# The second MLP product of a hybrid encoder block: seven Strassen block products in place of eight, on one Trainium2 core

## Chip, cores and metric

The kernel runs on one core of one Trainium2 chip. The metric is the device time of one execution in microseconds. Three runs of the kernel before took 856.59, 857.76 and 857.15 us; the median is 857.15 us.

## What is computed

The layer has 512 tokens and 1024 channels. A recurrent mixer and a sparse attention run side by side, their outputs are gated, added and projected, and the result is added to the input. Behind that stands the squared-ReLU MLP, which is what the change is about:

```python
D_MODEL = 1024; SEQ = 512; D_FF = 4 * D_MODEL
...
merged = gates[:, :, 0] * (y_rnn @ w_o_rnn) + gates[:, :, 1] * (y_attn @ w_o_attn)
x = x + merged @ w_out

h2 = rms_norm(x, norm2_w)
x = x + jnp.square(jax.nn.relu(h2 @ w_ff_in)) @ w_ff_out
```

All of it is float32. The second product has 512 x 4096 activations and 4096 x 1024 weights.

## The kernel before

**Precision.** TensorE multiplies in a rounded float32 type (fp32r). Every operand is split into a high part (ScalarE casts it) and a low part (VectorE subtracts the cast from the original), and one product of two operands is three matmuls: high by high, high by low, low by high (mm3, line 443). Weights are split in the same way when they arrive: unit (line 464) loads 128 x 1024 floats into a tile raw, ScalarE casts them into wh, and VectorE (or GpSimd) subtracts into wl. The pools hold 2 tiles raw, 5 wh and 5 wl (SLOTS, line 49).

**Layout.** Channels lie on the partitions and the 512 tokens along the free axis. A block of 128 output channels is one PSUM bank of 128 x 512, and the weights are the stationary operand (block, line 481).

**The MLP** (lines 923 to 947) runs in two halves of the hidden channels. In each half 16 blocks of the first product are made (24 matmuls of 512 columns each), ReLU is taken on ScalarE and the square on VectorE, and the result is split into hidh and hidl. Then for each of the 8 blocks of output channels 48 matmuls run over these 16 hidden blocks, and VectorE scales the bank by the inverse norm (a tile rb2 of 128 x 512) and adds it to x2, the residual. In the second half x2 goes out by DMA after that; its last block is cut into two halves of 256 tokens. The norm of a token is needed for all channels at once, so one fp32 matmul with a matrix of ones (line 935) spreads the sums over all partitions.

**What sets the order.** The program is a list of operations, and a planner (Plan, lines 118 to 339) puts them into one fixed order per engine with its own table of costs and numbers of buffers; each engine then works through its queue in order and waits at semaphores. A buffer is a slot with a tag. The change touches the tags a (67 tiles of 128 x 512), pt (4 tiles of 128 x 1664, which hold the transposed attention weights pth and ptl of a head, line 835), T and S (2 PSUM banks each) and acc (4 PSUM banks). DMAs of weights are issued by SyncE (SP), one after the other in its queue.

**Attention.** For each of 16 heads PE makes the scores, VectorE adds the bias, ScalarE takes the exponentials and the normalisation (norm, line 418), PE transposes the four tiles of weights (flip, line 449), they are cast and subtracted into pth and ptl, and PE multiplies them by the values. Matmuls of other products stand between these steps in PE's queue.

Of the kernel before, what the change touches and what calls it, by code (L numbers as in the profile page):

```python
# [11 lines left out]
F32 = mybir.dt.float32  # L12
F32R = mybir.dt.float32r
# [4 lines left out]
D = 1024  # L18
T = 512
# [325 lines left out]
def build(tc, out, xT, w_x, w_iq, w_vi, w_k, w_q, w_or, w_oa, w_o, w_f1, w_f2, w_bd, vec, nw):  # L345
# [22 lines left out]
    def val(x):  # L368
        return x.real() if isinstance(x, View) else x
# [68 lines left out]
    def mm(o, a, b, first, last, fp32=False):  # L438
        n = o.n
        cost = (4 if fp32 else 1) * n / 2.4 + 13.4 if n > 128 else 86  # L440
        plan.add("pe", cost, lambda: nc.tensor.matmul(val(o), lhsT=val(a), rhs=val(b), start=first, stop=last), [o], [a, b])  # L441

    def mm3(o, a, b, first, last):
        mm(o, a[0], b[0], first, False)
        mm(o, a[0], b[1], False, False)
        mm(o, a[1], b[0], False, last)

    def flip(o, a):
        plan.add("pe", 86, lambda: nc.tensor.transpose(val(o), val(a.f), val(ident)), [o], [a, ident])  # L449
# [28 lines left out]
        sub(l[:, 0:n], raw[:, 0:n], h[:, 0:n], "any")  # L478
        return h, l

    def block(src, x, parts=None, get=unit):

        w = [get(s_) for s_ in src]
        res = []
        for s in parts or [slice(0, T)]:
            o = P()[:, s]
            for k, x_ in enumerate(x):
                u = w[k // KT]
                mm3(o, (u[0][:, tok(k % KT)], u[1][:, tok(k % KT)]), (x_[0][:, s], x_[1][:, s]), k == 0, k == len(x) - 1)
            res.append((s, o))  # L490
        return res if parts else res[0][1]
# [41 lines left out]
    def tok(t):  # L533
        return slice(t * 128, (t + 1) * 128)
# [384 lines left out]
        x2w.append((h, l))  # L919

    rb2 = A("rb2")
    HALF = DFF // 256
    for half in range(2):
        hid = []
        for n in range(half * HALF, half * HALF + HALF):
            o = block([w_f1[n]], x2w)
            r_ = A("rel")
            act(r_, o, AF.Relu)  # L930
# [21 lines left out]
def pack(inputs):  # L952
    a = {k: np.asarray(v) for k, v in inputs.items()}
    w = a["w_in"][0]

    def cols(m):
        n = m.shape[1] // 128
        return m.reshape(KT, 128, n, 128).transpose(2, 1, 0, 3).reshape(n, 128, 1024)

    def rows(m, per):  # L960
        n = m.shape[1]
        return m.reshape(KT // per, per, 128, n).transpose(0, 2, 1, 3).reshape(KT // per, 128, per * n)

# [8 lines left out]
    p = {  # L972
        "xT": a["x"][0].T.reshape(KT, 128, T),
        "w_x": cols(np.concatenate([w[:, 0:2048], w[:, 4168:6216]], axis=1)),
        "w_iq": rows(w[:, 3584:4096], 1),
        "w_vi": rows(np.concatenate([w[:, 3328:3584], w[:, 4096:4168]], axis=1), 8)[0],
        "w_k": rows(w[:, 3072:3328], 4),
        "w_q": cols(w[:, 2048:3072]),
        "w_or": cols(a["w_o_rnn"][0]),
        "w_oa": cols(a["w_o_attn"][0]),  # L980
        "w_o": cols(a["w_out"][0]),
        "w_f1": cols(a["w_ff_in"][0]),
        "w_f2": a["w_ff_out"][0].reshape(4, KT, 128, 8, 128).transpose(3, 0, 2, 1, 4).reshape(8, 4, 128, 1024),
        "w_bd": bd.reshape(2, 128, 1024),
        "vec": np.concatenate([chan(a[k][0]) for k in (
            "norm1_w", "conv_w", "conv_b", "rg_ba", "rg_bx", "rg_lambda", "gate_b", "norm2_w")], axis=1),
        "nw": np.broadcast_to(np.concatenate([a[k][0] for k in ("q_norm_w", "k_norm_w", "idx_k_norm_w")]), (128, 192)),
    }
    return {k: np.ascontiguousarray(v) for k, v in p.items()}
# [11 lines left out]
```

## Time and profile before

| what | before |
|---|---|
| median of 3 runs | 857.15 us |
| the profiled execution, its own time | 856.84 us |
| its span, first to last instruction | 854.7 us |
| PE busy | 841.5 us, 98% |
| DVE (VectorE) busy | 513.9 us, 60% |
| ACT (ScalarE) busy | 440.9 us, 52% |
| DMA | 92.34 MB, mean 108 GB/s |

Shares are means over the whole span. A matmul is listed with its full duration, which overlaps the next one's, so how fast PE goes is read from the distance between two starts and not from durations or busy time. The lines of a helper (441 matmul, 449 transpose, 396 two-input operation of VectorE, 383 and 385 ScalarE) stand for many places in the program; the names of the tiles tell them apart.

### The profile page before, as it was taken

What the parts mean: (1) busy time and instruction counts of PE and PEld (TensorE: products, weight loads), DVE (VectorE), ACT (ScalarE), POOL (GpSimd) and SP (SyncE); (2) the same over time, 40 slices, a digit from 0 to 9 for tenths busy, and PEclk for the clock granted to TensorE, in tenths of its full rate; (3) what the DMA queues carried; (4) which work ended last, traced back from release to release, by engine and by line L of the source; (5) the groups of instructions that cost most, each with busy time, mean ns of one, the idle gap of its engine ahead of it and who ended that gap; (6) DMA issues with size and microseconds to landing.
All of it is one profiled execution on the core that took longest, in us unless ns stands there. A gap on an engine that the chain in (4) does not pass through costs nothing.

```text
span 854.7 us, 10592 instructions
## 1 busy us (share of the span) xinstructions
PE 841.5 (98%) x4004; PEld 703.6 (82%) x4004; DVE 513.9 (60%) x958; ACT 440.9 (52%) x756; POOL 113.2 (13%) x110
## 2 busy tenths in 40 slices
PE   9979999999999999999999999999999999999998
PEld 9968888888788888888788888888888888888887
DVE  7786989899647676857386556444333344443321
ACT  8668697699566575777734333443111244331110
POOL 1552224211031222122040000000000000000000
PEclk9989999999999999999999999999999999999999
DMA  7573778864322412121024332233333333333310
GB/s 264 163 197 81 167 155 194 196 150 119 99 74 74 158 53 74 50 75 49 26 81 140 101 99 96 91 91 96 97 97 99 98 99 99 99 98 124 120 54 25
DMA packets 27986, 92.34 MB, mean 108 GB/s; under 512 B 3232, under 2 KB 3616, under 8 KB 27936
## 3 DMA queue, kind: packets, MB, share of 16 engines
q1 hardware_dynamic: 21024, 66.51, 24.8%
q0 software_dynamic: 6912, 25.17, 13.2%
q8 instruction: 31, 0.51, 0.3%
q14 instruction: 19, 0.16, 0.1%
HBM read 89.57 MB, written 2.10 MB: 107 GB/s over the span
## 4 chain that ended last, share of the span: by engine, by line
PE 95%; ACT 2%; POOL 1%; issue 1%; DVE 1%; POOLq 0%; ACTq 0%
PE ps L441 93%; PE ps L449 2%; ACT xnh L383 0%; POOL wl L396 0%; ACT rel L385 0%; ACT sm L385 0%; ACT ikT L383 0%; POOL bdl L396 0%; DVE iks L396 0%; PE ps L813 0%; POOL cik L396 0%; ACT L385 0%; ACT pth L383 0%; DVE hl L396 0%; POOL wh L460 0%
## 5 line engine op out<-in xcount | busy, mean ns | idle before, releaser
L383 ACT CAST wh<-raw 128x1024 fp32r<-128x1024 f32 (+2 forms) x94 | 98.3, 1048 | 217.7 <-PE ps L441 196.0
L396 DVE TENSOR_TENSOR wl<-raw,wh 128x1024 fp32r<-128x1024 f32 (+1 forms) x91 | 110.8, 1218 | 123.0 <-ACT wh L383 122.2
L441 PE MATMUL ps<-xnh,wl 128*128 128x512 f32 x320 | 126.4, 395 | 0.0
L441 PE MATMUL ps<-xnl,wh 128*128 128x512 f32 x320 | 126.1, 394 | 0.0
L441 PE MATMUL ps<-xnh,wh 128*128 128x512 f32 x320 | 126.0, 394 | 0.0
L441 PE MATMUL ps<-hidl,wh 128*128 128x512 f32 (+1 forms) x272 | 102.4, 377 | 0.0
L441 PE MATMUL ps<-hidh,wl 128*128 128x512 f32 (+1 forms) x272 | 102.4, 377 | 0.0
L441 PE MATMUL ps<-hidh,wh 128*128 128x512 f32 (+1 forms) x272 | 102.4, 377 | 0.0
L441 PE MATMUL ps<-x2h,wh 128*128 128x512 f32 x256 | 100.0, 391 | 0.0
L441 PE MATMUL ps<-x2h,wl 128*128 128x512 f32 x256 | 99.6, 389 | 0.0
L441 PE MATMUL ps<-x2l,wh 128*128 128x512 f32 x256 | 99.6, 389 | 0.0
L441 PEld LDWEIGHTS ps<-xnl,wh 128*128 128x128 f32 x320 | 60.2, 188 | 11.9
L441 PEld LDWEIGHTS ps<-xnh,wl 128*128 128x128 f32 x320 | 60.2, 188 | 11.7
L441 PEld LDWEIGHTS ps<-xnh,wh 128*128 128x128 f32 x320 | 60.2, 188 | 11.3
L396 POOL TENSOR_TENSOR wl<-raw,wh 128x1024 fp32r<-128x1024 f32 (+1 forms) x18 | 45.4, 2523 | 155.2 <-PE ps L441 61.8
L441 PEld LDWEIGHTS ps<-hidh,wl 128*128 128x128 f32 x272 | 51.2, 188 | 9.4
L441 PEld LDWEIGHTS ps<-hidh,wh 128*128 128x128 f32 x272 | 51.2, 188 | 9.4
L441 PEld LDWEIGHTS ps<-hidl,wh 128*128 128x128 f32 x272 | 51.2, 188 | 9.3
L441 PEld LDWEIGHTS ps<-x2h,wh 128*128 128x128 f32 x256 | 48.0, 188 | 10.2 <-issue 0.2
L441 PEld LDWEIGHTS ps<-x2l,wh 128*128 128x128 f32 x256 | 48.1, 188 | 10.1 <-issue 0.2
L441 PEld LDWEIGHTS ps<-x2h,wl 128*128 128x128 f32 x256 | 48.0, 188 | 10.1
L396 DVE TENSOR_TENSOR y<-ps,rb 128x512 f32<-128x512 f32 (+1 forms) x17 | 11.2, 660 | 65.4 <-PE ps L441 65.4
(213 smaller groups left out, 1595.2 us busy)
## 6 DMA issues: line engine op xcount, KB each, us to landing
raw<-w_f SPq DMA_DIRECT2D x64, 512.0 KB, 3.5
wh<-w_x POOLq DMA_DIRECT2D x24, 512.0 KB, 5.1
wl<-w_x POOLq DMA_DIRECT2D x24, 512.0 KB, 5.5
raw<-w_q SPq DMA_DIRECT2D x8, 512.0 KB, 3.6
raw<-w_or SPq DMA_DIRECT2D x8, 512.0 KB, 3.5
raw<-w_x SPq DMA_DIRECT2D x8, 512.0 KB, 3.4
raw<-w_oa SPq DMA_DIRECT2D x8, 512.0 KB, 3.5
raw<-w_o SPq DMA_DIRECT2D x8, 512.0 KB, 3.5
```

The costliest lines, as they stand in the source:

```text
L383: nc.scalar.copy(val(o), val(a))
L396: return lambda: ENG[e].tensor_tensor(val(o), val(a), val(b), op=op)
L441: plan.add("pe", cost, lambda: nc.tensor.matmul(val(o), lhsT=val(a), rhs=val(b), start=first, stop=last), [o], [a, b])
L449: plan.add("pe", 86, lambda: nc.tensor.transpose(val(o), val(a.f), val(ident)), [o], [a, ident])
```

## The change

The first product stays as it is. The second is done in the other orientation and with fewer matmuls.

- The residual x2 is transposed on PE to token-major tiles xt (32 transposes of 128 x 128 into four-wide banks with the tag S, copied out by ScalarE). The inverse norm becomes one column of four numbers per partition (rs2); the ones matmul and the reciprocal of 128 x 512 go.
- The hidden channels are worked in four chunks of 8 blocks, which are 4 pairs (a, b). A pair gives a 2 x 2 grid: rows are token halves H1 and H2, columns are the blocks a and b. Strassen's sums of these quarters (s12, s34) are made on VectorE, and each of them is split into high and low parts. ScalarE now takes the square.
- The weights of a pair come as w_f2 rows (two DMAs into one tile w2 of tag pt, and one into b21 of tag a). Their sums are made in place on VectorE (tt on b12, b11, b21), and each operand is cast and subtracted into wh and wl just before its product (operands).
- A chunk has seven products in the order 1, 2, 6, 5, 7, 3, 4, of 24 matmuls each: 4 pairs, 2 token tiles, 3 matmuls. The activations are stationary, the weights move (512 columns). Each product fills or adds to two PSUM banks (R or V, tag acc), and after each put adds both banks, scaled by rs2, to xt with one VectorE operation per bank. Products 6, 7, 3 and 4 add onto banks that were already read by an earlier put.
- The output is stored token-major, 8 DMAs of 128 x 512 at the end.

```diff
-    rb2 = A("rb2")
-    HALF = DFF // 256
-    for half in range(2):
-        hid = []
-        for n in range(half * HALF, half * HALF + HALF):
-            o = block([w_f1[n]], x2w)
-            r_ = A("rel")
-            act(r_, o, AF.Relu)
-            tt(r_, r_, r_, ALU.mult, "any")
-            hid.append(split(r_, "hid"))
...
-        for c in range(KT):
-            src = [w_f2[c, 2 * half + u] for u in range(2)]
...
-            for s, o in block(src, hid, parts):
-                y_ = A("y2")[:, s]
-                tt(y_, o, rb2[:, s], ALU.mult)
-                tt(x2[c][:, s], x2[c][:, s], y_, ALU.add)
-                if half == 1:
-                    dma(out[c][:, s], x2[c][:, s])
+    xt = [[A("xt") for _ in range(2)] for _ in range(NT)]
+    for t in range(NT):
+        for d in range(2):
+            tp = P("S")
+            for c in range(4):
+                flip(tp[:, tok(c)], x2[4 * d + c][:, tok(t)])
+            act(xt[t][d], tp, either=True)
...
+    for t in range(NT):
+        mm(ss_ps[:, t:t + 1], sacc2[:, tok(t)], ones[:, 0:1], True, True, True)
...
+    def halves(src, cols):
+        h, l = cols
+        act(h, src, either=True)
+        sub(l, src, h)
+
+    def hidden(n):
+        o = block([w_f1[n]], x2w, unit, "T")
+        r_ = A("rel")
+        act(r_, o, AF.Relu)
+        act(r_, r_, AF.Square)
+        return r_
...
+    for ch in range(CHUNKS):
+        S, a22, w = [], [], []
+        for j in range(PAIRS):
+            a, b = (hidden((ch * PAIRS + j) * 2 + i) for i in range(2))
...
+            halves(a[:, H1], at)
+            tt(s12[:, H1], a[:, H2], b[:, H2], ALU.add)
+            tt(s12[:, H2], s12[:, H1], a[:, H1], ALU.subtract)
+            tt(s34[:, H1], a[:, H1], a[:, H2], ALU.subtract)
+            tt(s34[:, H2], b[:, H1], s12[:, H2], ALU.subtract)
+            pb, p12, p34 = two("ab"), two("s12"), two("s34")
+            for src, dst in ((b, pb), (s12, p12), (s34, p34)):
+                halves(src, dst)
...
+            raw = plan.tile(ab, [128, 1664], F32, "pt", "w2")
+            b21 = A("b21")
+            n = (ch * PAIRS + j) * 2
+            dma(raw[:, 0:1024], w_f2[n])
+            dma(b21, w_f2[n + 1][:, 0:512])
+            dma(raw[:, 1024:1536], w_f2[n + 1][:, 512:1024])
...
+        def product(i, o, B, first):
+            for j in range(PAIRS):
+                for p in range(2):
+                    mm3(o[p], cut(S[j][i], tok(p)), B[j], first and j == 0, j == PAIRS - 1, not first)
...
+        def put(i, d, o):
+            left[i, d] -= 1
+            for p in range(2):
+                t, x_ = 2 * i + p, xt[2 * i + p][d]
+                stt(x_, o[p], rs2[:, t:t + 1], x_, ALU.mult, ALU.add)
+                if left[i, d] == 0:
+                    dma(out[t][:, d * 512:d * 512 + 512], x_)
+
+        R, V = banks("acc"), banks("acc")
+        product(1, R, operands(0), True)
+        put(0, 0, R)
+        product(2, V, operands(2), True)
+        put(0, 0, V)
+        for b11, b12, b21, b22, _ in w:
+            tt(b12, b22, b12, ALU.subtract)
+            tt(b11, b12, b11, ALU.add)
+        product(6, R, operands(0), False)
+        put(0, 1, R)
+        for b11, b12, b21, b22, _ in w:
+            tt(b21, b21, b11, ALU.subtract)
+            tt(b11, b22, b11, ALU.subtract)
+        V = banks("acc")
+        product(5, V, operands(0), True)
+        put(1, 1, V)
+        t3b22 = []
...
+        product(7, R, [cut(u, slice(0, 512)) for u in t3b22], False)
+        put(1, 1, R)
+        product(3, V, [cut(u, slice(512, 1024)) for u in t3b22], False)
+        put(0, 1, V)
+        product(4, R, operands(2), False)
+        put(1, 0, R)
```

The planner orders the whole program anew. Three places show what moves.

PE at the last attention head (the last with pth and ptl; ps is a PSUM bank, sm the weights, ya the attention output by which the next product, w_oa, is fed). Before:

```order
L441 MATMUL ps_4278<-yal_3770,wh_3939 128x512
L441 MATMUL ps_4278<-yah_3756,wl_3958 128x512
L441 MATMUL ps_4278<-yah_4016,wh_3939 128x512
L449 MATMUL ps_4318<-ident_72,sm_4153 128x128 [waits DVE_49]
L449 MATMUL ps_4318<-ident_72,sm_4153 128x128 x3
L441 MATMUL ps_4278<-yal_4029,wh_3939 128x512
L441 MATMUL ps_4278<-yah_4016,wl_3958 128x512
L441 MATMUL ps_4278<-yah_4242,wh_3939 128x512
L441 MATMUL ps_4278<-yal_4246,wh_3939 128x512
L441 MATMUL ps_4278<-yah_4242,wl_3958 128x512
L441 MATMUL ps_4330<-pth_4295,vs_482 128x512 [waits Activation_49]
L441 MATMUL ps_4330<-ptl_4301,vs_482 128x512 [waits DVE_49]
```

After, from the end of head 15 of 16 on:

```order
L441 MATMUL ps_4315<-pth_4271,vs_627 128x128
L441 MATMUL ps_4315<-ptl_4280,vs_627 128x128
L450 MATMUL ps_4328<-ident_72,sm_4163 128x128 [waits PE_49,Activation_49]
L450 MATMUL ps_4332<-ident_72,sm_4171 128x128 [waits PE_49,Activation_49]
L450 MATMUL ps_4332<-ident_72,sm_4171 128x128
L450 MATMUL ps_4343<-ident_72,sm_4178 128x128 [waits DVE_49]
L450 MATMUL ps_4343<-ident_72,sm_4178 128x128 x2
L450 MATMUL ps_4348<-ident_72,sm_4187 128x128 [waits DVE_49,Activation_49]
L450 MATMUL ps_4348<-ident_72,sm_4187 128x128 x3
L441 MATMUL ps_4356<-pth_4335,vs_482 128x512 [waits Activation_49]
L441 MATMUL ps_4356<-ptl_4340,vs_482 128x512 [waits DVE_49]
```

Before, matmuls of the next product (ya) stand between the last head's transposes (ident, sm) and its product with the values (vs); after, none stands there: the transposes follow the fifteenth head directly and the product with the values follows them.

PE at the start of the MLP, where the output projection (mg) ends and the first block of the first MLP product (x2h, x2l) begins. Before:

```order
L441 MATMUL ps_4835<-mgl_4582,wh_4677 128x512
L441 MATMUL ps_4835<-mgh_4573,wl_4689 128x512
L441 MATMUL ps_4874<-x2h_4607,wh_4716 128x512 [waits DVE_49,Activation_49]
L441 MATMUL ps_4874<-x2l_4615,wh_4716 128x512
L441 MATMUL ps_4874<-x2h_4607,wl_4728 128x512
L441 MATMUL ps_4874<-x2h_4647,wh_4716 128x512
L441 MATMUL ps_4874<-x2l_4659,wh_4716 128x512
```

After:

```order
L441 MATMUL ps_4877<-mgh_4624,wl_4729 128x512
L450 MATMUL ps_4916<-ident_72,x_196 128x128
L450 MATMUL ps_4916<-ident_72,x_2831 128x128
L450 MATMUL ps_4916<-ident_72,x_2835 128x128
L450 MATMUL ps_4916<-ident_72,x_2955 128x128
L450 MATMUL ps_4922<-ident_72,x_2963 128x128 [waits DVE_49]
L450 MATMUL ps_4922<-ident_72,x_2968 128x128 [waits DVE_49]
L450 MATMUL ps_4922<-ident_72,x_2975 128x128 [waits DVE_49]
L441 MATMUL ps_4926<-x2h_4658,wh_4756 128x512 [waits Activation_49]
L441 MATMUL ps_4926<-x2l_4670,wh_4756 128x512
L441 MATMUL ps_4926<-x2h_4658,wl_4768 128x512
L441 MATMUL ps_4926<-x2h_4687,wh_4756 128x512
```

The first 12 of the 32 transposes of x2 stand there and among the following 25 matmuls of that block; each group of four waits for a bank that ScalarE has to empty.

VectorE late in a chunk. Before, in the second half of the second product (y and x are the scaling and the addition):

```order
L396 TENSOR_TENSOR y_6743<-ps_6676,rb_4957 128x512 [waits PE_49]
L396 TENSOR_TENSOR x_2831<-x_2831,y_6743 128x512 [waits DVE_49]
L396 TENSOR_TENSOR wl_6753<-raw_6697,wh_6739 128x1024 [waits DMAHW2_49,Activation_49]
L396 TENSOR_TENSOR wl_6782<-raw_6725,wh_6774 128x1024 [waits DMAHW3_49,PE_49,Activation_49]
L396 TENSOR_TENSOR y_6808<-ps_6741,rb_4957 128x512 [waits PE_49]
L396 TENSOR_TENSOR x_2837<-x_2837,y_6808 128x512 [waits DVE_49]
L396 TENSOR_TENSOR wl_6818<-raw_6762,wh_6804 128x1024 [waits DMAHW5_49,Activation_49]
L396 TENSOR_TENSOR wl_6847<-raw_6790,wh_6839 128x1024 [waits DMAHW6_49,PE_49,Activation_49]
```

After, in the second chunk from the last split of the operands of products 7 and 3 on (xt rows are put, w is the weight tile of the third chunk, b is b21):

```order
L396 TENSOR_TENSOR wl_6155<-w_5519,wh_6142 128x1024 [waits Activation_49]
L424 SCALAR_TENSOR_TENSOR xt_4991<-ps_6118,rs_4993,xt_4991 128x512 [waits PE_49]
L424 SCALAR_TENSOR_TENSOR xt_5011<-ps_6127,rs_4993,xt_5011 128x512 [waits PE_49]
L396 TENSOR_TENSOR wl_6180<-b_4049,wh_6169 128x512 [waits Activation_49]
L396 TENSOR_TENSOR wl_6180<-b_4055,wh_6169 128x512 [waits Activation_49]
L396 TENSOR_TENSOR w_6124<-w_6124 128x512 [waits DMAHW4_49,DMAHW3_49,DVE_49]
L396 TENSOR_TENSOR w_6147<-w_6147 128x512 [waits DMAHW6_49,DMAHW5_49,DVE_49]
L424 SCALAR_TENSOR_TENSOR xt_4991<-ps_5987,rs_4993,xt_4991 128x512 [waits DVE_49,PE_49]
L424 SCALAR_TENSOR_TENSOR xt_5011<-ps_5993,rs_4993,xt_5011 128x512 [waits DVE_49,PE_49]
L396 TENSOR_TENSOR w_6157<-w_6157 128x512 [waits DMAHW7_49,DMAHW0_49]
L396 TENSOR_TENSOR wl_6219<-b_4066,wh_6212 128x512 [waits Activation_49]
L396 TENSOR_TENSOR wl_6219<-b_4075,wh_6212 128x512 [waits Activation_49]
```

Where before two splits of weights and two operations on a finished bank alternated, there are now splits, puts and sums on weights, and the sums on w wait for DMAs (DMAHW) of the next chunk's weights while puts and splits of the running chunk stand behind them.

In SP's queue the loads of w2 and b21 are issued as soon as slots are free: two w2 tiles before the first heads of the attention, nine b21 tiles in its course, and the next two w2 tiles when the last two heads have released their pt slots, ahead of the last block of w_oa. From the second chunk on the four w2 tiles of a chunk are loaded when the splits for products 7 and 3 of the chunk before have read the old ones.

## Rows read from the trace of the kernel before

**Rows 1.** The page's part 1: busy us of each engine (share of the span) xinstructions.

```profile
PE 841.5 (98%) x4004; PEld 703.6 (82%) x4004; DVE 513.9 (60%) x958; ACT 440.9 (52%) x756; POOL 113.2 (13%) x110
```

**Rows 2.** Chain that ended last: start us, us, what.

```profile
428.07 422.76 PE ps L441 x1907
```

**Rows 3.** Busy us by engine over the MLP: window, length, PE, PEld, DVE, ACT, POOL.

```profile
501.00:851.00 350.00, 349.81 (x1587) 291.09 (x1585) 140.67 (x161) 99.89 (x126) 1.29 (x1) 1.00 0.30 93
```

**Rows 4.** Timeline of PE, 512 columns, then 256: start us, us, engine, what.

```profile
504.82 0.39 PE L441 MATMUL ps<-x2h,wl 128*128 128x512 f32 x1
...
511.62 0.39 PE L441 MATMUL ps<-x2h,wl 128*128 128x512 f32 x1
...
849.58 0.28 PE L441 MATMUL ps<-hidh,wh 128*128 128x256 f32 x1
...
850.53 0.28 PE L441 MATMUL ps<-hidh,wl 128*128 128x256 f32 x1
```

**Rows 5.** Timeline of PE around a group of four transposes, earlier stage.

```profile
79.78 0.60 PE L449 MATMUL ps<-ident,ks 128*128 128x128 f32 x4
...
80.45 0.40 PE L441 MATMUL ps<-xnh,wl 128*128 128x512 f32 x1
```

**Rows 6.** Groups by form: ScalarE's cast of a PSUM bank: busy us, mean ns of one.

```profile
L383 ACT CAST pth<-ps 128x512 fp32r<-128x512 f32 x16 | 9.4, 585 | 3.9 <-PE ps L449 3.7
```

**Rows 7.** Sums of squares on PE: timeline with 512 columns; tile sacc, one column.

```profile
511.84 1.02 PE L441 MATMUL ps<-sacc,ones 128*128 128x512 f32 x2
...
512.93 0.39 PE L441 MATMUL ps<-x2l,wh 128*128 128x512 f32 x1
...
L441 PE MATMUL ps<-ones,sacc x8: 166/250/250, 22.8 to 23.5; 128*128 128x1 f32 x8
```

**Rows 8.** Groups of VectorE by form (tile y: ns min/median/max): mean ns of one.

```profile
L396 DVE TENSOR_TENSOR wl<-raw,wh 128x1024 fp32r<-128x1024 f32 x89 | 108.8, 1223 | 123.0 <-ACT wh L383 122.2 <-PE ps L441 0.6
L396 DVE TENSOR_TENSOR rel<-rel 128x512 f32<-128x512 f32 x32 | 21.9, 685 | 0.0
L396 DVE TENSOR_TENSOR hidl<-rel,hidh 128x512 fp32r<-128x512 f32 x31 | 21.5, 693 | 21.4 <-ACT hidh L383 21.4
L396 DVE TENSOR_TENSOR y<-ps,rb x17: 424/692/692, 600.0 to 850.9; 128x512 f32<-128x512 f32 x15, 128x256 f32<-128x256 f32 x2
L424 DVE SCALAR_TENSOR_TENSOR x2l<-x,vt,x2h 128x512 fp32r<-128x512 f32 x8 | 6.0, 748 | 0.8 <-ACT x2h L385 0.8
```

**Rows 9.** DMA issues: size of one, median us from issue to landing.

```profile
raw<-w_f SPq DMA_DIRECT2D x64, 512.0 KB, 3.5
out<-x SPq DMA_DIRECT2D x7, 256.0 KB, 2.0
out<-x SPq DMA_DIRECT2D x2, 128.0 KB, 1.7
```

**Rows 10.** Timeline of PE between the last two attention heads.

```profile
418.59 0.27 PE L441 MATMUL ps<-ptl,vs 128*128 128x128 f32 x1
...
425.01 0.40 PE L441 MATMUL ps<-pth,vs 128*128 128x512 f32 x1
```

**Rows 11.** Groups by form: the steps of a head between scores and values.

```profile
L418 ACT ACTIVATE sm<-sm,st 128x512 f32<-128x512 f32 x16 | 11.5, 720 | 0.0
L383 ACT COPY yt<-ps 64x512 f32<-64x512 f32 x16 | 9.3, 581 | 16.7 <-PE ps L441 16.7
L396 DVE TENSOR_TENSOR ptl<-ps,pth 128x512 fp32r<-128x512 f32 x16 | 11.0, 688 | 3.4 <-ACT pth L383 3.3
```

**Rows 12.** Timeline of the end: the last bank and the store.

```profile
850.85 0.42 DVE L396 TENSOR_TENSOR y<-ps,rb 128x256 f32<-128x256 f32 x1 [4.87 <-PE ps L441]
851.31 0.42 DVE L396 TENSOR_TENSOR x<-x,y 128x256 f32<-128x256 f32 x1
851.76 0.33 SPq L436 DMA_DIRECT2D out<-x  x1
```

**Rows 13.** A VectorE operation of 512 columns that runs beside GpSimd's work.

```profile
L396 DVE TENSOR_TENSOR qsql<-qsq,qsqh 128x512 fp32r<-128x512 f32 x8 | 7.7, 972 | 1.0 <-ACT qsqh L383 0.9
```

More of the change, by code (lines that the diff above doesn't have):

```diff
@@ L436, in dma, with mm, mm3 @@
         plan.add("sp", n * 128 * 4 / 268.0, lambda: nc.sync.dma_start(val(o), val(src)), w, r)
-    def mm(o, a, b, first, last, fp32=False):
+    def mm(o, a, b, first, last, fp32=False, more=False):
         n = o.n
         cost = (4 if fp32 else 1) * n / 2.4 + 13.4 if n > 128 else 86
[L441 to L446, printed above, removed]
+        plan.add("pe", cost, lambda: nc.tensor.matmul(val(o), lhsT=val(a), rhs=val(b), start=first, stop=last, skip_group_check=more), [o], [a, b])
+    def mm3(o, a, b, first, last, more=False):
+        mm(o, a[0], b[0], first, False, more=more)
+        mm(o, a[0], b[1], False, False, more=more)
+        mm(o, a[1], b[0], False, last, more=more)
     def flip(o, a):
@@ L479, in unit, with block @@
         return h, l
-    def block(src, x, parts=None, get=unit):
+    def block(src, x, get=unit, tag="acc"):
         w = [get(s_) for s_ in src]
[L484 to L491, printed above, removed]
+        o = P(tag)
+        for k, x_ in enumerate(x):
+            u = w[k // KT]
+            mm3(o, (u[0][:, tok(k % KT)], u[1][:, tok(k % KT)]), x_, k == 0, k == len(x) - 1)
+        return o
     def natural(pieces, per, n, x):
@@ new lines, in build @@
+    for t in range(NT):
[4 more added lines that the diff above has]
+            act(xt[t][d], tp, either=True)
+    rs2 = small(4, "rs2")
+    ss_ps = P("T")
+    for t in range(NT):
+        mm(ss_ps[:, t:t + 1], sacc2[:, tok(t)], ones[:, 0:1], True, True, True)
+    ts(rs2, ss_ps[:, 0:4], 1.0 / D, EPS, ALU.mult, ALU.add)
+    dve(4, lambda: nc.vector.reciprocal(val(rs2), val(rs2)), [rs2], [rs2])
@@ new lines, in build, with two, cut @@
+    PAIRS, H1, H2 = 4, slice(0, 256), slice(256, 512)
+    def halves(src, cols):
[8 more added lines that the diff above has]
+        return r_
+    def two(p, dt=F32R):
+        return A(p + "h", dt), A(p + "l", dt)
+    def cut(x, s):
+        return x[0][:, s], x[1][:, s]
+    CHUNKS = DFF // (256 * PAIRS)
+    left = {(0, 0): 2 * CHUNKS, (0, 1): 2 * CHUNKS, (1, 1): 2 * CHUNKS, (1, 0): CHUNKS}
@@ new lines, in build, with operands, banks @@
+    for ch in range(CHUNKS):
+        S, a22, w = [], [], []
+        for j in range(PAIRS):
+            a, b = (hidden((ch * PAIRS + j) * 2 + i) for i in range(2))
+            s12, s34 = A("s12"), A("s34")
+            if j % 2 == 0:
+                a11 = two("a11")
+            at = cut(a11, (H1, H2)[j % 2])
+            halves(a[:, H1], at)
[6 more added lines that the diff above has]
+                halves(src, dst)
+            S.append({1: at, 2: cut(pb, H1), 4: cut(pb, H2), 5: cut(p12, H1), 6: cut(p12, H2), 7: cut(p34, H1), 3: cut(p34, H2)})
+            raw = plan.tile(ab, [128, 1664], F32, "pt", "w2")
[4 more added lines that the diff above has]
+            dma(raw[:, 1024:1536], w_f2[n + 1][:, 512:1024])
+            w.append((raw[:, 0:512], raw[:, 512:1024], b21, raw[:, 1024:1536], raw[:, 512:1536]))
+        def operands(which):
+            res = []
+            for j in range(PAIRS):
+                if j % 2 == 0:
+                    u = [plan.tile(ab, [128, 1024], F32R, t_, t_) for t_ in ("wh", "wl")]
+                v = cut(u, slice(j % 2 * 512, j % 2 * 512 + 512))
+                halves(w[j][which], v)
+                res.append(v)
+            return res
+        def product(i, o, B, first):
+            for j in range(PAIRS):
+                for p in range(2):
+                    mm3(o[p], cut(S[j][i], tok(p)), B[j], first and j == 0, j == PAIRS - 1, not first)
+        def banks(tag):
+            return [P(tag) for _ in range(2)]
+        def put(i, d, o):
[22 more added lines that the diff above has]
+        t3b22 = []
+        for j in range(PAIRS):
+            u = [plan.tile(ab, [128, 1024], F32R, t_, t_) for t_ in ("wh", "wl")]
+            halves(w[j][4], u)
+            t3b22.append(u)
+        product(7, R, [cut(u, slice(0, 512)) for u in t3b22], False)
[4 more added lines that the diff above has]
+        put(1, 0, R)
@@ L982, in pack @@
         "w_f1": cols(a["w_ff_in"][0]),
-        "w_f2": a["w_ff_out"][0].reshape(4, KT, 128, 8, 128).transpose(3, 0, 2, 1, 4).reshape(8, 4, 128, 1024),
+        "w_f2": a["w_ff_out"][0].reshape(32, 128, 1024),
         "w_bd": bd.reshape(2, 128, 1024),
@@ L995 @@
     aps = {k: nc.dram_tensor(k, v.shape, mybir.dt.from_np(v.dtype), kind="ExternalInput").ap() for k, v in arrays.items()}
-    out = nc.dram_tensor("out", (KT, 128, T), F32, kind="ExternalOutput").ap()
+    out = nc.dram_tensor("out", (NT, 128, D), F32, kind="ExternalOutput").ap()
     with tile.TileContext(nc) as tc:
@@ L999 @@
     r = run_bass_kernel_spmd(nc, [arrays], core_ids=[0])
-    return np.ascontiguousarray(np.asarray(r.results[0]["out"]).reshape(D, T).T)[None]
+    return np.ascontiguousarray(np.asarray(r.results[0]["out"]).reshape(T, D))[None]
```

6 lines of the change are left out of this document (removed).

## The prediction

> **What bounds the kernel now.** I read the page's busy times first, then the chain that ended last, then the windows of the MLP, then PE's timeline. PE is busy 98% of the span [rows 1]. The chain says the same in order of time: its last piece is one run of PE over 422.76 us, from 428.07 us on, with no other engine in it [rows 2]. In the window from 501 to 851 us, which is the MLP, PE is busy 349.81 of 350.00 us at a clock of 1.00, VectorE 140.67, ScalarE 99.89 and GpSimd 1.29 us [rows 3]. So here time is PE's instructions, and the other engines have room.
>
> What one matmul costs is the distance between starts. From 504.82 to 511.62 us there are 30 steps of 512 columns: 6.80 / 30 = 0.2267 us; from 849.58 to 850.53 us 8 steps of 256 columns: 0.119 us [rows 4]. As a check, the first product has 32 x 24 = 768 matmuls, the second 720 of 512 columns and 96 of 256: 1488 x 0.2267 + 96 x 0.119 = 348.7 us, and the sums' matmul below adds 0.9: 349.6 of the 350 us of the window. Nothing stalls there.
>
> **The change, part by part, against the profiled execution** (856.84 us, of which 854.7 are the span; it lies 0.3 us under the median of 857.15).
>
> A. *Matmuls of the second product.* Removed 720 x 0.2267 + 96 x 0.119 = 174.6 us. Added 4 chunks x 7 products x 24 = 672 of 512 columns: 152.3 us. **-22.3 us.** I take the same distance for the new form, since 512 columns move in both; bounds for it stand under the third rival.
>
> B. *Transposes of x2.* 32, in groups of four. In the earlier stage a group of four starts at 79.78 us and the second matmul behind it at 80.45: 0.67 us for four transposes and one matmul of 0.227, so 0.44 per group [rows 5]. 8 x 0.44 = **+3.5 us**. The banks are emptied by eight copies on ScalarE; its cast of such a bank takes 0.585 us [rows 6]. They must follow x2's own work there. By hand, with 0.75 us for VectorE's operation on x2's last tile and 0.6 to 0.7 for each of ScalarE's two on it: the copies begin some 2.2 us after the projection's end and go on until 7; PE asks for the third bank after 3.4 us, and then for one about each 0.9 us. So nothing waits. If all the copies were uncovered it would be 8 x 0.585 = 4.7 us more.
> The Trainium skill (TensorE: Matmul & The Clock Gate, Part 4: PE-mode transpose) gives some 275 ns for a transpose in a kernel's context; by that alone B would be 32 x 0.275 = 8.8 us, an estimate, and the sum 5.3 us more. The trace shows the same 0.27 us as a duration but overlapped, so I keep 3.5.
>
> C. *Norm.* The fp32 matmul with 512 columns goes: 511.84 to 512.93 us holds it and one matmul, so 0.86 us. Four with one column come; the eight records of such four start between 22.8 and 23.5 us, so about 0.8 us [rows 7]. **0.** The reciprocal of 512 columns goes from VectorE, which waits anyway.
>
> D. *VectorE and ScalarE in a chunk.* PE needs (8 + 7) x 24 x 0.2267 = 81.6 us for a chunk. VectorE needs, by [rows 8]: 8 splits of first-product weights x 1.223 = 9.8; 4 double splits (products 7 and 3) x 1.223 = 4.9; 20 single splits x 0.693 = 13.9; 16 sums on weights x 0.685 = 11.0; 12 splits of activations x 0.693 = 8.3; 20 operations of 256 columns x 0.424 = 8.5; 14 puts x 0.748 = 10.5 (the form with a column per partition). Sum 66.9 us, 82% of PE's. It had 140.67 us in the whole MLP and now has 4 x 66.9 = 268. ScalarE takes the square from it and stays lower still, about half of PE's time. Covered on the whole; what matters is the place. The tightest run is products 5, 7 and 3 of a chunk (3 x 24 x 0.2267 = 16.3 us), where VectorE's queue has 6 puts 4.5, 3 double splits 3.7, 4 splits 2.8, 4 weight sums 2.7 and one first-product split 1.2: 14.9 us. Each operand then lies ready 2.5 us or more before PE asks for it; the nearest is the first split of product 5, some 2.9 us after product 2 ends, needed after 5.4. **0** if its DMAs come in time.
> Those DMAs are the unknown. VectorE's queue has the sums on the next chunk's w2 tiles in this run, ahead of the put of product 7, of the last two splits of product 4 and of a split for the next chunk. The tiles' slots come free only with the double splits, about 1 us after product 5 begins and then one per 1.2 us or so. A tile is 512 + 256 KB. At 3.5 us for 512 KB one at a time [rows 9] it is 5.2 us a tile: the third lands 16.7 us after product 5 began and the split behind its sum ends near 18.5, before PE needs it (19.0); the fourth lands at 22, the next chunk's first split ends near 24, and PE asks for it at 21.8 + 0.5. That is a stall of up to 2 us at each of three chunk boundaries, 6 us in all. At the other end, transfers overlap and cost nothing; 3.5 us contain the latency, and SP issues the next transfer without waiting for the one before. I take 0 and keep 6.
>
> E. *The attention's end.* The order shows the same matmuls there, but the filler that stood in the last head now stands before it. In the trace of before, 6.4 us lie between the last matmul of head 15 and the first with the values of head 16 (418.59 to 425.01), with 21 matmuls of filler in it (4.8 us) and 1.1 us of transposes [rows 10]. Without filler PE waits for the chain of the head: the copy of the fifteenth head's output 0.581, the fourth normalisation 0.720, the last cast 0.585 [rows 6], the subtraction 0.688 [rows 11], and shorter ones of the first three tiles among them. By hand the product with the values can go on some 3.5 to 4 us after the fifteenth head, and PE has 1.1 us of transposes in that: a hole of 2.5 us. Bounds: 0, if the chain has run ahead by then, since the filler that moved up gave it 4.8 us; 5.3 us, if all but the transposes is exposed. **+2.5 us**, between the two. The w2 tiles take two of the four pt slots during the attention; in the order the first 13 heads keep their sequence, so I count nothing for that.
>
> F. *The end.* Before, 256 columns were scaled and added in 0.42 + 0.42 us and 128 KB stored in 1.7 us [rows 9, 12]. Now the last of two puts of 0.748 begins when the last matmul ends (the other bank is done 3 matmuls earlier), so about 1.05 us after it, and 256 KB go in 2.0. **+0.5 us** (0 to 1).
>
> Sum: -22.3 + 3.5 + 0 + 0 + 2.5 + 0.5 = -15.8, so 856.84 - 15.8 = **841.0 us**.
>
> **Rivals.**
> 1. *VectorE's queue stands behind the DMAs at the chunk boundaries* (D's upper end). For it: the queue is in order, the sums are ahead of needed splits, and 3 MB are asked for within 5 us. Against: DMA is busy 0.30 of the MLP's window [rows 3]. Time 843 to 847.
> 2. *The attention's end costs nothing* (E at 0): the projections reached there earlier make up for the hole. For it: PE's work up to that point is the same in both. Against: the last two heads follow each other without cover. Time 838.5.
> 3. *The change doesn't do what it says*: the new form of matmul, whose two banks alternate every three and are added to after VectorE has read them, comes at a longer distance than 0.2267. For it: no row of the second product has that form. Against: the loads of the stationary side, of the same size in both, take 703.6 / 4004 = 0.18 us each and stay under the distance [rows 1]. The gain is gone at 0.2267 + 15.8 / 672 = 0.250 us. Halfway there the time is 849.
> 4. *Slower: VectorE becomes the bound.* Its 66.9 us a chunk need only grow by 28% to 85.5 (81.6 + 15.8 / 4), and nothing is left. Price: a subtraction of 512 columns that takes 0.693 us takes 0.972 where GpSimd works beside it [rows 8, 13], a factor of 1.40. With all of VectorE at that, a chunk takes 93.8 us, and 4 x (93.8 - 81.6) = 49 us go on top: 890. Against: GpSimd had 1.29 us of work in the MLP [rows 3], and the new order gives it two subtractions of the first product's weights there.
> The Trainium skill (SBUF — State Buffer, Who interferes with whom) states that VectorE and GpSimd share a port pair by an exclusive lock, and the loser stands still for a whole instruction. The trace agrees in direction, 0.972 for 0.693 us; for GpSimd's two subtractions it makes some 5 us at most, an estimate, and 846 if none of it were covered.
>
> **How the numbers follow.** Forecast (839.5 to 843.5) 0.62; rival 1 0.14; rival 2 and a little below 0.14; rival 3 0.05, partly slower; rival 4 0.05. The range runs from 837, below rival 2 by what B and F could be too high, to 849, above rival 1 by 2 us of E. Under 0.2% (1.7 us) a measurement of this kernel can't tell from no change. Faster 0.93, within 0.2% 0.02, slower 0.05.
>
> **What would show it.** Distance of 0.227 us between starts of matmuls with s12, s34, ab or a11 as stationary (A); a group of x2's transposes at 0.44 us (B); VectorE near 67 us a chunk, and PE with no idle time between the first and last matmul of the MLP (D); a hole of 2 to 4 us before the last head's product with the values (E). The forecast is wrong if PE waits for wl or wh tiles in the chunks, by more than a few us in all, or if the part before the MLP moves by more than 6 us.

## The result: 845.44 us, and the profile after

The changed kernel takes 845.44 us (median of four runs, 844.21 to 846.35) against 857.24 for the kernel before (a fourth run of it, 857.32 us, joins the three above): ratio 0.9862, 95% interval 0.9845 to 0.9879. It is 1.4% faster. The forecast was 841.0 with a range of 837 to 849, so the time lies inside the range, 4.4 us above the forecast. The profiled execution took 844.21 us.

The page's busy times, to be put beside [rows 1] (busy us, share of the span, instructions):

```profile
PE 824.0 (98%) x3898; PEld 687.5 (82%) x3898; DVE 610.5 (72%) x1172; ACT 507.9 (60%) x892; POOL 114.2 (14%) x110
```

The last pieces of the chain that ended last, against [rows 2] (start us, us, what):

```profile
423.57 3.78 PE ps L441 x19
...
434.02 73.06 PE ps L441 x321
...
515.39 321.92 PE ps L441 x1420
837.33 1.43 DVE xt L424 x2
```

PE still carries the chain to the end. But the long run that began at 428.07 us before begins at 434.02 now: 6 us are lost ahead of it. The windows say where (length; then busy us of PE, PEld, DVE, ACT, POOL; granted clock; DMA):

```profile
85.00:358.00 273.00, 272.85 (x1296) 225.14 (x1295) 212.53 (x483) 199.03 (x345) 59.56 (x52) 1.00 0.50 127
358.00:375.00 17.00, 14.41 (x70) 11.35 (x69) 12.60 (x22) 10.95 (x25) 4.17 (x2) 0.90 0.31 93
...
420.00:434.02 14.02, 10.49 (x58) 8.27 (x57) 5.91 (x12) 9.19 (x23) 0.00 (x0) 1.00 0.05 4
434.02:506.92 72.90, 72.90 (x322) 60.31 (x323) 51.46 (x58) 28.77 (x38) 9.98 (x4) 1.00 0.44 144
...
598.00:679.60 81.60, 81.60 (x362) 67.57 (x361) 59.30 (x93) 40.99 (x64) 2.40 (x1) 1.00 0.28 90
679.60:761.20 81.60, 81.60 (x362) 67.57 (x361) 59.56 (x93) 41.11 (x64) 2.40 (x1) 1.00 0.28 91
```

Two chunks of the MLP (the last two rows) hold PE at 81.60 of 81.60 us: no stall. The losses are in two places of the attention. At 358 to 375 us PE is idle for 2.6 us and the clock falls to 0.90; at 420 to 434 us it is idle for 3.5 us. In the kernel before, the first place was full:

```profile
358.00:376.00 18.00, 18.00 (x97) 14.85 (x97) 13.54 (x26) 13.04 (x29) 2.42 (x1) 1.00 0.19 59
```

The books close. From 110.69 to 434.02 us are 323.33 us; the same piece of work (from the same matmul to the same matmul), from 111.16 to 428.07 us, took 316.91 before: 6.42 us more. PE's new waits in it, from the timeline of after (start us, us, what, idle before and what ended it):

```profile
362.14 0.52 PE L450 MATMUL ps<-ident,sm 128*128 128x128 f32 x3 [1.03 <-DVE ptl L396]
369.05 0.50 PE L441 MATMUL ps<-xnh,wh 128*128 128x512 f32 x1 [0.97 <-ACT qsq L385]
370.15 0.52 PE L450 MATMUL ps<-ident,sm 128*128 128x128 f32 x3 [0.60 <-DVE ptl L396]
428.92 1.05 PE L450 MATMUL ps<-ident,sm 128*128 128x128 f32 x7 [1.23 <-DVE ptl L396]
430.65 0.50 PE L441 MATMUL ps<-pth,vs 128*128 128x512 f32 x1 [0.68 <-ACT pth L383]
431.37 0.50 PE L441 MATMUL ps<-ptl,vs 128*128 128x512 f32 x1 [0.23 <-DVE ptl L396]
434.02 0.50 PE L441 MATMUL ps<-yah,wh 128*128 128x512 f32 x1 [1.40 <-DVE yt L396]
```

The first three make 2.60, the next three 2.14. The last, 1.40, stood before the same matmul in the kernel before too. The clock of 0.90 over 17 us takes 1.7 us: from 371.1 to 374.5 us, about 3.4 us, it was at half. Sum: 6.4.

What held up VectorE before the first of these waits is seen in the timelines of GpSimd (POOL) and VectorE:

```profile
357.41 2.40 POOL L396 TENSOR_TENSOR wl<-raw,wh 128x1024 fp32r<-128x1024 f32 x1 [24.41 <-DVE wh L389]
```

```profile
356.48 0.69 DVE L389 CAST wh<-raw 128x1024 fp32r<-128x1024 f32 x1
...
358.27 2.08 DVE L389 CAST wh<-raw 128x1024 fp32r<-128x1024 f32 x1 [0.38 <-PE ps L441]
360.27 1.40 DVE L389 CAST hl<-ps 64x512 fp32r<-64x512 f32 x2
361.70 0.62 DVE L396 TENSOR_TENSOR ptl<-ps,pth 128x128 fp32r<-128x128 f32 x2
```

The same cast takes 0.69 us at 356.48 and 2.08 us at 358.27, where it ends soon after GpSimd's subtraction (357.41 + 2.40 = 359.81). The subtraction ptl, for which PE waits, stands three instructions behind it.

At the second and third wait it is PE's own queue that differs. Between its groups of two and of three transposes (ident, sm) the kernel before runs eight matmuls of another product (xnh, xnl); the changed kernel runs only one of them there, that of 369.05 us above, and two short ones of the scores, and so it waits. The kernel before:

```profile
367.41 0.38 PE L449 MATMUL ps<-ident,sm 128*128 128x128 f32 x2
...
369.50 0.49 PE L449 MATMUL ps<-ident,sm 128*128 128x128 f32 x3
```

The transfers themselves are not under way at either place. In SP's queue no load of w_ff_out (w_f) is issued between these two lines of the changed kernel, nor from 407.26 to 432.55 us:

```profile
297.00 0.33 SPq L436 DMA_DIRECT2D b<-w_f  x1
...
396.97 3.26 SPq L436 DMA_DIRECT2D b<-w_f  x5
```

### The profile page after: what moved, and what is told of

Same layout as the page of the kernel before. It is cut to its first block, busy times and chain, and to the rows that moved or that the text cites. A ratio compares the mean times of both kernels' runs of the same rounds, so it can differ in the third digit from the quotient of the medians.

```text
span 842.4 us, 10752 instructions
## 1 busy us (share of the span) xinstructions
PE 824.0 (98%) x3898; PEld 687.5 (82%) x3898; DVE 610.5 (72%) x1172; ACT 507.9 (60%) x892; POOL 114.2 (14%) x110
## 4 chain that ended last, share of the span: by engine, by line
PE 95%; ACT 2%; DVE 1%; POOL 1%; issue 1%; POOLq 0%; ACTq 0%
PE ps L441 92%; PE ps L450 3%; ACT xnh L383 0%; POOL wl L396 0%; ACT rel L385 0%; ACT ikT L383 0%; DVE ptl L396 0%; POOL bdl L396 0%; DVE iks L396 0%; DVE yt L396 0%; DVE xt L424 0%; PE ps L811 0%; POOL cik L396 0%; ACT sm L385 0%; ACT L385 0%
## 5 line engine op out<-in xcount | busy, mean ns | idle before, releaser
L383 ACT CAST wh<-raw 128x1024 fp32r<-128x1024 f32 (+2 forms) x62 | 64.6, 1045 | 73.9 <-PE ps L441 36.9
L396 POOL TENSOR_TENSOR wl<-raw,wh 128x1024 fp32r<-128x1024 f32 (+1 forms) x19 | 47.7, 2515 | 450.4 <-ACT wh L383 333.5
L396 DVE TENSOR_TENSOR wl<-raw,wh 128x1024 fp32r<-128x1024 f32 (+2 forms) x58 | 70.1, 1214 | 19.3 <-ACT wh L383 18.0
L383 ACT CAST wh<-w 128x512 fp32r<-128x512 f32 (+1 forms) x64 | 45.7, 726 | 54.7 <-PE ps L441 51.1
L396 DVE TENSOR_TENSOR wl<-w,wh 128x512 fp32r<-128x512 f32 (+1 forms) x64 | 50.8, 820 | 18.6 <-ACT wh L383 18.6
L424 DVE SCALAR_TENSOR_TENSOR xt<-ps,rs,xt 128x512 f32<-128x512 f32 x56 | 39.6, 747 | 25.8 <-PE ps L441 25.8
L385 ACT ACTIVATE sm<-sm,st,cq 128x128 f32<-128x128 f32 (+1 forms) x64 | 41.4, 649 | 9.1 <-DVE st L396 9.1
L383 ACT CAST wh<-b 128x512 fp32r<-128x512 f32 x32 | 19.0, 618 | 43.0 <-PE ps L441 43.0
L385 ACT ACTIVATE rel<-ps 128x512 f32<-128x512 f32 (+2 forms) x56 | 30.1, 549 | 23.6 <-PE ps L441 23.4
L396 DVE TENSOR_TENSOR ptl<-ps,pth 128x128 fp32r<-128x128 f32 (+1 forms) x64 | 30.0, 487 | 12.1 <-ACT pth L383 11.4
```

The lines of the kernel that those rows point to most:

```text
L424: lambda: nc.vector.scalar_tensor_tensor(val(o), val(a), val(s), val(b), op0=op0, op1=op1),
```

## The experiments

Two theories stood against each other. A: the loads of w_ff_out, for which tile slots in the attention are free earlier, make the planner deal casts, subtractions and filler there in another order, and that order loses 6.4 us; Strassen's products themselves have nothing to do with it. B: the loss belongs to the new work or its transfers wherever it stands.

**The loads later.** Each load of w_ff_out may be planned only after the last head's output is split.

```
-    def dma(o, src):
+    def dma(o, src, gate=None):
...
-        plan.add("sp", n * 128 * 4 / 268.0, lambda: nc.sync.dma_start(val(o), val(src)), w, r)
+        op = plan.add("sp", n * 128 * 4 / 268.0, lambda: nc.sync.dma_start(val(o), val(src)), w, r)
+        if gate is not None:
+            op.after.add(gate)
...
             ya.append(split(yt, "ya"))
+            gate = plan.ops[-1]
...
-            dma(raw[:, 0:1024], w_f2[n])
+            dma(raw[:, 0:1024], w_f2[n], gate)
...
```

Expected: 

> Only change: the loads of w_ff_out may be planned only after the last head's output is split (an edge in the plan, no wait on the chip). PE, VectorE and GpSimd then have the order of the kernel before up to the attention's end. Theory A (the early loads fill the shared buffers, so the planner deals the attention's casts and subtractions differently, and that costs 4.6 us near 360 us and about 1.5 us between the last two heads): attention ends near 428 us instead of 434, the MLP stays at 331 us, the time falls to 838 to 839.5, ratio to before about 0.978. Rival B (the loss is in the MLP's neighbourhood or in the transfers themselves, whatever the order): attention ends near 434 or the MLP starts with stalls of its own, time 844 to 846. Rival C (the loads, now later, arrive late for the first chunk): attention at 428, but the MLP longer than 331 by the 3 to 5 us that the loads of one chunk take, time 841 to 844.

Measured: 841.24 us, ratio to before 0.9806 (0.9790 to 0.9821). The attention is whole again: from 113.06 to 429.96 us are 316.90 us, as before. Here the loads are issued from 420.63 us on, beside the last head; the DMA share is 0.46 from 415 to 431 us, and PE is idle for 1.53 us there, as before, so the transfers beside it cost nothing. (The stretch starts later because this execution had a granted clock of 0.93 from 15 to 40 us, 1.7 us; the changed kernel's had 1.00.) But a new wait stands in the output projection, which the expectation had not named:

```profile
461.41 0.50 PE L443 MATMUL ps<-mgh,wl 128*128 128x512 f32 x1 [1.47 <-DVE wl L396]
```

VectorE's own timeline shows why:

```profile
459.53 0.69 DVE L424 SCALAR_TENSOR_TENSOR g<-g,ps 128x512 f32<-128x512 f32 x1 [2.65 <-PE ps L443]
460.14 1.22 DVE L396 TENSOR_TENSOR wl<-raw,wh 128x1024 fp32r<-128x1024 f32 x1
```

The weight's subtraction, which PE wants, is queued behind an operation that waits 2.65 us for PE. In SP's queue the twelve loads of the first chunk and six more now stand ahead of the output projection's loads; that the planner deals the subtraction late for this reason is a reading of the order, which the next run tests. A holds; its size was reached only in part. (The expectation's 4.6 and 1.5 us for the two places were rougher readings; the books above give 4.3 and 2.1.)

**The loads later still.** The gate moves behind the last block of the output projection.

```
         stt(r_, o, 0.5, r_, ALU.mult, ALU.add)
+        gate = plan.ops[-1]
...
-            dma(raw[:, 0:1024], w_f2[n])
+            dma(raw[:, 0:1024], w_f2[n], gate)
...
```

Expected: 

> As the kernel with the gate, but the gate stands behind the last block of the output projection, so that all four engines and SP keep the order of the kernel before up to the first MLP chunk. Theory A (the whole shortfall against the sum is what the early loads do to the order of the work ahead of the MLP): attention's last projection starts near 428 us, the 1.47 us wait at 461 us that the first gate left is gone, 72.9 us from there to the first transpose, MLP 330.7 us: 838.5 to 839.5 us, ratio about 0.979 or lower, 1.5 to 2 us under the first gate. Rival (the first chunk's blocks now come late, about 3 MB in 12 us and 64 sums of blocks pushed into the chunk): PE waits in the first chunk, MLP 332 to 336 us, time 840 to 844.

Measured: 838.78 us (838.36 to 839.02), ratio 0.9786 (0.9773 to 0.9800): the best version, 6.7 us under the changed kernel's median. Its windows (attention, the place of the first waits, last heads, both projections, first chunk):

```profile
85.00:358.00 273.00, 272.85 (x1297) 225.09 (x1296) 214.85 (x483) 197.78 (x344) 61.43 (x52) 1.00 0.47 123
358.00:376.00 18.00, 18.00 (x98) 14.88 (x97) 13.53 (x26) 13.06 (x29) 2.42 (x1) 1.00 0.19 61
415.00:428.04 13.04, 11.53 (x58) 8.54 (x58) 5.37 (x10) 8.55 (x21) 0.00 (x0) 1.00 0.00 0
428.04:500.94 72.90, 72.90 (x322) 60.31 (x323) 50.52 (x56) 28.64 (x38) 9.99 (x4) 1.00 0.34 110
500.94:592.00 91.06, 91.06 (x423) 75.82 (x422) 65.39 (x103) 46.81 (x74) 0.00 (x0) 1.00 0.43 156
```

PE and the clock are full from 358 to 376 us, the hole between the last heads is the old one of 1.5 us, and the first chunk does not wait for its later loads, though the DMA share rises to 0.43. The wait in the output projection is gone, and the eight matmuls between the transposes near 368 us are back. This shows that the whole loss, at both places, came from the loads' place in the plan. B falls. Not separated is which early loads do it, the w2 tiles (tag pt) or the nine b21 tiles (tag a).

**The slow cast alone.** The changed kernel's plan is kept row for row; the one cast of 2.08 us is issued on ScalarE.

```
+    wide = []
...
+        def on_vector():
+            wide.append(o.n == 1024)
+            (nc.scalar.copy if o.n == 1024 and sum(wide) == 11 else nc.vector.tensor_copy)(val(o), val(a))
...
-                   lambda: nc.vector.tensor_copy(val(o), val(a)))
+                   on_vector)
```

Expected: 

> The changed kernel with its plan kept row for row, but the one 128x1024 cast that took 2.08 us beside GpSimd's subtraction (at 358 us) is emitted on ScalarE, where such a cast takes about 1.05 us. Theory A (that cast, held up by GpSimd, delayed VectorE's chain, PE's three waits of 2.6 us followed, and then 3.4 us at the half clock): the waits at 362 to 371 us and the half-clock stretch go, the attention ends near 430 us, time 840.5 to 842. Rival B (the heads there are short of work in that order anyway): the waits stay within 1 us of 2.6, the clock falls again, time 844 to 845. Rival D (the waits go, the fall of the clock comes all the same): time about 843.

Measured: 844.78 us (843.13 to 847.45), ratio 0.9852 (0.9827 to 0.9876): not told apart from the changed kernel by its time. The trace does tell them apart: the first wait is gone, the other two are not, and the clock falls as before (the windows from 355 us on):

```profile
355.00:362.00 7.00, 7.00 (x41) 5.86 (x39) 5.81 (x11) 5.82 (x15) 4.45 (x2) 1.00 0.14 40
362.00:376.00 14.00, 12.44 (x61) 10.20 (x59) 8.87 (x18) 9.22 (x19) 0.30 (x1) 0.88 0.31 94
```

```profile
367.94 0.50 PE L445 MATMUL ps<-xnh,wh 128*128 128x512 f32 x1 [0.97 <-ACT qsq L386]
369.04 0.52 PE L454 MATMUL ps<-ident,sm 128*128 128x128 f32 x3 [0.59 <-DVE ptl L400]
```

So the cast beside GpSimd's subtraction is worth 1.03 of the 6.4 us. I had taken it for the cause of all three waits (theory A); that was wrong. For the other two rival B holds: in that order the heads are short of work for PE, as the one matmul left of eight between the transposes shows.

**Eight plain products in the new orientation.** With the first gate; Strassen's sums and products are replaced by the eight block products.

```
...
-        product(1, R, operands(0), True)
...
+        for d in range(2):
+            R, V = banks("acc"), banks("acc")
+            B = operands((0, d))
+            product(0, 0, R, B, True)
+            product(1, 0, V, B, True)
+            B = operands((1, d))
+            product(0, 1, R, B, False)
+            put(0, d, R)
+            product(1, 1, V, B, False)
+            put(1, d, V)
```

Expected: 

> The same token-major form and the same late loads as the kernel with the gate, but with the eight plain block products in place of Strassen's seven: 4 chunks x 24 matmuls of 512 columns more, no sums of blocks. At 0.2267 us a matmul that is +21.8 us on the kernel with the gate: 860 to 861 if the gate gives 838.5, so slower than before by about 3 to 4 us (the transposes). Rival: the token-major form alone carries part of the gain (its matmuls run closer together with fewer operands to prepare), then 850 to 856; or Strassen's sums cost PE hidden waits that vanish here, then under 858.

Measured: 862.18 us, ratio 1.0058 (1.0039 to 1.0076). The MLP, first transpose to the start of the last matmul, of this kernel and then of the one with the first gate:

```profile
503.09:855.53 352.44, 352.44 (x1577) 292.31 (x1575) 123.39 (x160) 125.41 (x198) 0.00 (x0) 1.00 0.22 73
```

```profile
504.66:835.34 330.68, 330.68 (x1480) 274.20 (x1479) 234.42 (x370) 165.92 (x262) 4.80 (x2) 1.00 0.23 78
```

The difference is 21.76 us, which is 96 x 0.2267 to the second decimal. The orientation alone gains nothing (it costs the transposes); the gain is the dropped eighth product. PE has no idle time in either, so the 111 us of VectorE's extra work are hidden.

**How well they are hidden.** Dummy VectorE sums of 512 columns are added to each pair (12, 4, 8), with the first gate; their results are not used.

```
...
+            for _ in range(12):
+                tt(pad, b, b, ALU.add)
             for src, dst in ((b, pb), (s12, p12), (s34, p34)):
                 halves(src, dst)
...
```

Expected with 12: 

> The kernel with the gate plus 12 dummy VectorE sums of 512 columns in every pair: 48 x 0.685 = 32.9 us more VectorE work in a chunk, on 59.3 measured, so 92 us against PE's 81.6. If the cover is VectorE's spare time (theory A: 22 us a chunk), the time rises by about 10.5 us a chunk, with the last chunk's end lighter: +30 to +45 us, and a chunk takes 91 to 94 us with VectorE above 95% busy. Rival: work of VectorE reaches PE by its latency, not its sum, then a chunk takes 100 us or more (+75 to +130 us); other rival: the sums slip in anywhere and nothing changes (0 to +5 us).

Expected with 4: 

> The kernel with the first gate plus 4 dummy VectorE sums of 512 columns in every pair: 16 x 0.685 = 11 us a chunk, on 59.3. With 12 a pair a chunk took about 108 us with VectorE 87% busy and PE's waits in the second half of the chunk, where each product's operands come from a chain of differences, casts and subtractions. Theory by the sum (VectorE 70 of 81.6): no wait, MLP 331 us, 840 to 842. Theory by the chain (VectorE must get ahead of PE in the first half of a chunk, and has little lead): waits of 2 to 6 us a chunk already, 850 to 865.

Expected with 8: 

> The same with 8 dummy sums a pair: 32 x 0.685 = 22 us a chunk, VectorE 81 of PE's 81.6. By the sum: at the edge, 0 to 5 us a chunk, 840 to 860. By the chain: between the kernel with 4 and that with 12, about 10 to 20 us a chunk, 880 to 915.

Measured: 949.85 us with 12 (ratio 1.1067, 1.1047 to 1.1088), 858.94 with 4 and 891.87 with 8 (one run each). So 11, 22 and 33 us of VectorE work a chunk cost 18, 51 and 109 us in all over the first gate's 841.24. The sum over a chunk (70 of 81.6 us with 4) said nothing would be lost; that theory falls, and with 12 its range of 30 to 45 was far too low. The rival ranges held all three times (75 to 130 more with 12; 850 to 865 with 4; 880 to 915 with 8). With 4, the third chunk in two parts, the hidden blocks and then the products:

```profile
673.00:717.00 44.00, 44.00 (x196) 36.44 (x195) 33.59 (x50) 22.90 (x37) 4.97 (x2) 1.00 0.30 96
717.00:757.00 40.00, 37.37 (x164) 30.32 (x163) 36.32 (x59) 16.81 (x28) 0.00 (x0) 1.00 0.22 77
```

VectorE has 10 us to spare in the first part and 3.7 in the second, and PE waits in the second. In all four chunks the long wait (1.30 us in the first, 2.51 in the others) is for the low part of a weight operand against s12h; in the third chunk:

```profile
743.98 0.50 PE L443 MATMUL ps<-wl,s12h 128*128 128x512 f32 x1 [2.51 <-DVE wl L396]
```

In VectorE's timeline of the changed kernel, second chunk, the second set of sums on the weights (b<-b,w) is worked in between the sums of the last blocks, ahead of the first put (with the first gate alone it is so too):

```profile
629.48 0.69 DVE L396 TENSOR_TENSOR b<-b,w 128x512 f32<-128x512 f32 x1
...
641.90 1.40 DVE L424 SCALAR_TENSOR_TENSOR xt<-ps,rs,xt 128x512 f32<-128x512 f32 x2
```

With 4 dummies, in the same chunk, it comes after the first puts:

```profile
644.27 1.40 DVE L424 SCALAR_TENSOR_TENSOR xt<-ps,rs,xt 128x512 f32<-128x512 f32 x2
...
650.73 1.29 DVE L396 TENSOR_TENSOR b<-b,w 128x512 f32<-128x512 f32 x2
```

There a product takes PE only 24 x 0.2267 = 5.4 us. So the idle time over a chunk doesn't measure the cover; what counts in these traces is how far ahead VectorE is at the end of the hidden blocks. With 4, PE's waits in the MLP are 9 us; about 5 us more go to stretches at the half clock (granted clock 0.96 and 0.93 in two of eight windows over the MLP), and the rest was not traced. These runs do not show that VectorE lacks the time: the dummies also make the planner deal anew (it gives GpSimd six subtractions of the MLP's weights instead of two), and whether another order could use the first part's idle 10 us was not tried.

## Why the prediction was right, and where it was not

- **A and B** (-22.3 and +3.5) and **C** (0). Right. From its first matmul or transpose to the start of the last matmul, the MLP took 500.96 to 850.53 = 349.57 us before and 506.92 to 837.58 = 330.66 after: -18.9, for -18.8 forecast. PE is busy all through both (the kernel before, then the changed one):

```profile
500.96:850.53 349.57, 349.57 (x1586) 291.04 (x1585) 140.52 (x160) 99.91 (x126) 1.29 (x1) 1.00 0.30 93
```

```profile
506.92:837.58 330.66, 330.66 (x1481) 274.20 (x1479) 234.58 (x370) 165.89 (x262) 4.81 (x2) 1.00 0.24 78
```

The new matmul comes at the old distance, and the transposes at the forecast one:

```profile
510.35 0.60 PE L450 MATMUL ps<-ident,x 128*128 128x128 f32 x4
510.71 0.48 PE L441 MATMUL ps<-x2h,wl 128*128 128x512 f32 x1
511.03 0.60 PE L450 MATMUL ps<-ident,x 128*128 128x128 f32 x4
...
837.35 0.39 PE L441 MATMUL ps<-wl,abh 128*128 128x512 f32 x1
837.58 0.39 PE L441 MATMUL ps<-wh,abl 128*128 128x512 f32 x1
```

From 510.35 to 511.03 us are 0.68; less a matmul's 0.23 that is 0.45 a group, for 0.44. Rival 3 is out.

- **D** (0). Right in the result: PE does not wait in the chunks, and the DMA bound of 6 us (rival 1) was not touched. The measured time lies where rival 1 put it, 843 to 847, but that is chance: its mechanism did not act. Sized wrong: VectorE is busy 59.6 us a chunk, not 66.9. The durations in one chunk add up to 65.2, since GpSimd took one of the eight first-product splits; the rest is that the records of back-to-back operations overlap, 0.61 us from start to start for durations of 0.69, which a sum of the durations in [rows 8] counts twice:

```profile
616.12 0.69 DVE L396 TENSOR_TENSOR w<-w 128x512 f32<-128x512 f32 x1
616.73 0.69 DVE L396 TENSOR_TENSOR wl<-w,wh 128x512 fp32r<-128x512 f32 x1
```

And wrong in what it would take: rival 4 put the point from which the gain is lost at 85.5 us a chunk. Four dummy sums a pair, at some 70 us a chunk, already lose it, if the plan that came with them is taken as it is.

- **E** (+2.5). This step failed, in the sentence "in the order the first 13 heads keep their sequence, so I count nothing for that". The attention cost 6.4 us: 2.1 between the last two heads, near the 2.5 forecast [rows 10], and 4.3 at 358 to 375 us that I had counted as nothing. The w2 loads hold two of the four pt slots there. What changes is not which head comes when, but what stands between a head's steps: a slow cast ahead of VectorE's subtraction at the first wait, and one matmul in place of eight between PE's transposes at the next two. Both gates undo both parts at once, so both come from the loads' place in the plan: with the later gate the kernel takes 838.78, and the sum without E is 856.84 - 18.3 = 838.5. The prediction's own sign of an error here, a part before the MLP that moves by more than 6 us, was missed by a hair: 500.96 to 506.92 us is 5.96. The range held because it had room above, not because E was right.

- **F** (+0.5). Right: the last matmul starts at 837.58 and the span ends at 842.4, 4.8 us; before 850.53 and 854.7, 4.2 us.

The rival on the port lock had the right mechanism in the wrong place. The Trainium skill (SBUF — State Buffer, Who interferes with whom) lets VectorE and GpSimd share a port pair by an exclusive lock. The trace agrees: 2.08 for 0.69 us, in the attention. The price in the prediction was misread, though. The 0.972 us of [rows 13] is the mean of eight operations whose median is 0.694; only two of them ran beside a subtraction of GpSimd, and they took 2.46 us (below) and 1.18 us. So 1.40 is no factor for an operation beside GpSimd, and the 890 us worked out from it has no ground:

```profile
269.59 2.40 POOL L396 TENSOR_TENSOR wl<-raw,wh 128x1024 fp32r<-128x1024 f32 x1 [13.62 <-DVE wh L389]
```

```profile
270.08 2.46 DVE L396 TENSOR_TENSOR qsql<-qsq,qsqh 128x512 fp32r<-128x512 f32 x1
```

## What to carry to other kernels

When a planner deals the instructions, price the whole region in which a new load or tile can become live, on every engine's queue, and not only the stage that is rewritten; an edge in the plan that keeps new loads out of a tuned stage cost nothing here and gave back 6.7 us. Whether a side engine's work is hidden can't be read from its idle time over a whole turn of a loop: read busy shares per part of the turn, and how far the side engine is ahead when the main engine begins to ask for its results faster. And a cause seen beside a loss (the slow cast) is worth what its removal brings, here 1.0 of 6.4 us.

## What the hardware showed beyond expectation

- Three VectorE operations of 0.69 us alone that began while GpSimd subtracted all ended about 0.54 us after that subtraction did: the cast of 128 x 1024 in the changed kernel (2.08 us) at 360.35 us against 359.81, and two subtractions of 128 x 512 in the kernel before, one of 2.46 us at 272.54 against 271.99 and one of 1.18 us at 324.68 against 324.14. In these three the delay followed what was left of GpSimd's operation and was no factor on VectorE's own time.
- After PE's waits of 0.97 and 0.6 us near 368 to 370 us, the granted clock fell to the lower level, 1.2 GHz, for about 3.4 us, in the changed kernel and in the one with the cast moved. After larger waits from 428 to 434 us in the changed kernel it stayed at 1.00 (the window above). With 4 dummies it fell towards the end of two of PE's waits of 2.51 us, those that end at 657.60 and 828.86 us, and not at the one that ends at 743.98. What decides is open.
- Adding 11 us a chunk of VectorE work cost PE more than its 9 us of waits, since about 5 us of the half clock came on top.
